# Retention's projections by seven half-block products in a stage of their own, and page keys gathered one unit ahead

## The chip, the cores and the metric

The kernel runs on one core of one Trainium2 chip. The core has five engines that work at the same time and wait for one another by semaphores: TensorE (PE in the profile, with its weight loads shown apart as PEld), VectorE (DVE), ScalarE (ACT), GpSimd (POOL) and SyncE (SP), which here only issues transfers. Each engine takes its own instructions strictly in their order. The metric is the time of one execution in microseconds on the device; smaller is better.

## What is computed

One step of a hybrid decoder layer on 1056 tokens: 1024 of a prompt and 32 of decoding (8 sequences of 4). All of it is float32. The part that matters here, cut from the reference:

```python
z = rmsnorm(x, ln_w) @ w_in                       # (1056, 1024) @ (1024, 9920)
rq, rk, rv, rg, cq, ckv, kr, mg, ga, gb = split(z)  # 1024, 1024, 2048, 2048, 384, 256, 64, 1024, 1024, 1024
rq = rope(rq by 4 heads of 256, pos)
rk = rope(rk by 4 heads of 256, pos) * 256 ** -0.5
rv = rv by 4 heads of 512
# retention, prompt: 8 chunks of 128 tokens per head, a state of 256 x 512 carried from chunk to chunk
scores = (q k^T) * decay_mask
o      = scores v + (q s_prev) * q_decay
s_new  = decay * s_prev + (k * k_decay)^T v
# latent attention of the decoding tokens: each sequence reads its 8192 past keys through a page table
c_past = cache_ckv[pt].reshape(-1, 256); r_past = cache_krope[pt].reshape(-1, 64)
p      = softmax([ql c_past^T + qr r_past^T, new tokens]);  o_lat = p [c_past, c_new]
```

Then come gates (`silu(rg)`, `silu(mg)`, `sigmoid(ga)`, `sigmoid(gb)`), three further projections, the prompt's latent attention and a last norm.

## The kernel before

**A product.** Float32 operands are split in two parts, high (`hi`) and low (`lo`), and `mac` (lines 262 to 268) multiplies them by three matmuls: high by high, high by low, low by high. `gemm` (line 270) makes one output tile of 128 columns of `w_in` by all 1056 tokens: three thirds of 352 tokens, each with 8 slices of the 1024 inputs, so 8 x 3 x 3 = 72 matmuls 352 wide, and it yields a cost of 0.441 after each `mac`. `load_w` fetches the tile's weights through two raw buffers (`wr`, 512 elements wide), casts them to `wh` on ScalarE or GpSimd and takes the low part `wl` on VectorE (`lo_of`, line 197); `wh` and `wl` have two buffers each. The normalised input `xn` stays in memory, 8 slices by high and low, until the projections are done.

**The stages.** In order: the input norm and the latents; the queries of the decoding tokens; the page attention (`page_attention`, line 672); retention (line 958 on); the prompt's latent attention; the last projections. The projections of the gates don't have a stage. They are a generator, `fill` (line 421), and `beside` (line 127) pours its matmuls between those of another stage in proportion to that stage's progress, counted in the costs that it yields; `woven` mixes two generators by their shares until both are used up. `fill` before: 8 tiles `ga`, 8 `gb`, 16 `rg`, 3 `mg` and the 4 `v` tiles of head 0, 39 in all.

**What sets the order.** The program is not run as it is written down. A planner takes all instructions with their dependences and buffers and sets each engine's order from its own estimate of times: the earlier one in the text has the higher priority, and a later one goes ahead where an engine would otherwise be free. On the chip that order is fixed, right or wrong. Buffers of one tag are handed on when their last reader is done.

**Page attention.** There are 16 units: two groups of four sequences, each by eight steps of 1024 keys (`past_keys`, line 612). A unit gathers its keys with 16 indirect transfers from GpSimd's queue (`gather`, line 579: two of the rotary keys into `rr` and two of the latent keys into `craw` for each sequence; each moves 128 rows). `craw` has buffers for two units under one tag, `rr` for one. Then 20 transposes on VectorE (`kt`, line 634, eight buffers, so two of five steps), 320 small score matmuls into one bank group `sc` (line 640), a maximum, an exponential on ScalarE, eight transposes, and the product with the keys (line 667). The unit yields 6.0 after its gathers, 12 in the scores, and 10.5 after.

**Retention.** q and k of head 0 are made first (`head_qk`), then for each head its v (`head_vg`), and then the head's recurrence (`prompt_chunks`, eight chunks with `front` and `back`) and its decoding state (`sample_state`) woven with q and k of the next head; beside the last head go five `mg` tiles. The rotation of q and k is done at the evacuation (lines 739 to 750). q, k and v of a head stay in memory, but for v of head 0, which goes through DRAM (`vD`).

Of the kernel before, what the change touches and what calls it, by code (L numbers as in the profile page):

```python
# [9 lines left out]
F32 = mybir.dt.float32  # L10
# [150 lines left out]
def decode_step(ctx: ExitStack, tc: tile.TileContext, A: dict, O: dict):  # L161
# [57 lines left out]
    vD = [dram.tile([P, NT], F32, tag=f"v{f}", name=f"v{f}") for f in range(4)]  # L219
# [197 lines left out]
    def chain(*gs):  # L417
        for g_ in gs:
            yield from g_

    fill = chain(gate_tiles(C_GA, gaD, range(8), AF.Copy), gate_tiles(C_GB, gbD, range(8), AF.Copy),
                 gate_tiles(C_RG, [t[:, f, :] for t in gtD for f in range(4)], range(16), AF.Silu), gate_tiles(C_MG, mgD, range(3), AF.Silu),
                 gate_tiles(C_RV, vD, range(4), AF.Copy))
# [53 lines left out]
    def big(name, shape, rows_=P):  # L477
        return p3.tile([rows_, *shape], F32, tag="craw", name=name, bufs=2 * NSEQ)
# [17 lines left out]
    def sample_queries():  # L496
# [11 lines left out]
        wk = big("wk", (2, HM, NOPE))  # L508
# [3 lines left out]
        qs = big("qq", (1536,))[:NR].rearrange("p (h d) -> p h d", h=HM)  # L512
        qq = big("qq", (768,))
# [19 lines left out]
        wkT = big("wkT", (HM, KL))  # L533
# [45 lines left out]
    def gather(b, jj, c, r):  # L579

        for i in range(NK):
            at_ = b * (NPG // 4) + NK * jj + i
            off = bass.IndirectOffsetOnAxis(ap=idx[:, at_:at_ + 1], axis=0)
            pool.indirect_dma_start(out=r[:, i], out_offset=None, in_=rows_r, in_offset=off)  # L584
            pool.indirect_dma_start(out=c[:, i], out_offset=None, in_=rows_c, in_offset=off)  # L585
# [26 lines left out]
    def past_keys(g, jj, st):  # L612
# [16 lines left out]
        for n, j in enumerate(steps):  # L629
            kt = []  # L630
            for s in range(NSEQ):
                t = ring("kt").rearrange("p (j k) -> p j k", j=2)
                src = keys[s][:, :, 32 * j:32 * j + 64] if j < 8 else rope[s]
                dve.transpose(t.rearrange("p j (n r) -> p n j r", r=32), src.rearrange("p n (j r) -> p n j r", r=32))  # L634
                kt.append(t)
            for i in range(2):
# [32 lines left out]
        dve.scalar_tensor_tensor(out=acc, in0=acc, scalar=corr, in1=pv[:, :KL], op0=ALU.mult, op1=ALU.add)  # L669
        yield 1.0  # L670

    def page_attention():
        state = [{}, {}]
        yield from new_tokens(0, state[0])
        for g in range(2):
# [5 lines left out]
            for jj in range(NPG // 4 // NK):  # L681
                yield from past_keys(g, jj, state[g])
# [36 lines left out]
    lph.close()  # L719

# [5 lines left out]
    tok = slots(p4, "tok", 8)  # L726
    cosR, sinR = (p4.tile([P, NT], F32, name=n) for n in ("cosR", "sinR"))
    sp.dma_start(cosR, A["ropeR"][:, 0, :])
    sp.dma_start(sinR, A["ropeR"][:, 1, :])
    lg = _log_g()  # L730

    def head_qk(h, X):
        for name, col in (("q", C_RQ), ("k", C_RK)):
            dst = X[name] = [(tok if h % 2 else qk4)(f"{name}{m}", dt=F32) for m in range(2)]

            def first(j, ps, sl, dst=dst):
                act.copy(dst[0][:, sl], ps)

            def second(j, ps, sl, dst=dst):
                x = wst.tile([P, TH], F32, tag="gev", name="rx", bufs=2)  # L740
                act.copy(x, ps)
                c, s = cosR[:, sl], sinR[:, sl]
                x0, x1 = dst[0][:, sl], dst[1][:, sl]
# [740 lines left out]
```

## Time and profile before

| | |
|---|---|
| median of 3 runs (lowest, highest) | 2253.39 us (2249.23, 2253.68) |
| the profiled execution: its time, its span | 2248.48 us, 2246.7 us |
| mean granted TensorE clock | 0.996 |
| TensorE busy in the span | 2192.1 us, 98% |
| VectorE, ScalarE, GpSimd busy | 1207.9, 709.8, 509.9 us |
| DMA traffic | 303.65 MB, mean 135 GB/s |

The profile's rows name a line, an engine, an operation, `out<-in` by the program's tile names with partitions x elements, and a count; then busy time, the mean of one in ns, and the engine's idle time before them with what ended it (`<-`). A timeline row is start, duration, engine, line. In rows of matmuls the duration is a model and neighbours overlap. A row by stretch gives the stretch, its length, the busy time of each engine with its count, the granted clock, the share of DMA time and GB/s. The page attention fills 204 to 806 us of the span, retention 806 to 1425.

### The profile page before, as it was taken

To read this page: it belongs to the slowest core of one execution; us is meant where nothing else is said; L and a number is where in the kernel's file an instruction comes from. 1 tells how busy PE (TensorE), PEld (TensorE's weight loads), DVE (VectorE), ACT (ScalarE), POOL (GpSimd) and SP (SyncE) were. 2 spreads that over 40 slices of the span, in tenths; PEclk is the share of its full clock that TensorE was granted. 3 is DMA by queue.
4 is the path that set the end of the run, shared out by engine and by line. 5 is a ranking of instruction groups with operands and counts; after the bars stand their busy time and mean duration, and the time that the engine had idled before them with its cause. 6 is when DMAs were issued, how large, how long until landed. Compare 5 with 4: busy or idle time off the path is not lost.

```text
span 2246.7 us, 45040 instructions
## 1 busy us (share of the span) xinstructions
PE 2192.1 (98%) x18482; PEld 1975.0 (88%) x18482; DVE 1207.9 (54%) x2624; ACT 709.8 (32%) x1532; POOL 509.9 (23%) x682
## 2 busy tenths in 40 slices
PE   8899999999999999999999999999999999999997
PEld 7898888888888899798798779888887999999997
DVE  5414454444544438728638447767767344454465
ACT  6312112222322123222222122355456332222243
POOL 2224434344444114203203102122222000000021
PEclk9999999999999999999999999999999999999999
DMA  8446565656565442532613753200110453333243
GB/s 234 131 148 247 184 223 174 227 183 222 182 232 178 153 135 59 165 99 66 212 49 95 237 162 87 81 23 24 37 46 27 149 192 106 96 94 107 87 141 114
DMA packets 293391, 303.65 MB, mean 135 GB/s; under 512 B 29760, under 2 KB 242048, under 8 KB 293184
## 3 DMA queue, kind: packets, MB, share of 16 engines
q1 hardware_dynamic: 268608, 216.86, 31.3%
q0 software_dynamic: 24576, 83.90, 10.8%
q8 instruction: 145, 2.38, 0.4%
q14 instruction: 62, 0.51, 0.1%
HBM read 234.76 MB, written 65.94 MB: 134 GB/s over the span
## 4 chain that ended last, share of the span: by engine, by line
PE 82%; DVE 7%; issue 6%; POOL 3%; ACT 2%; DMA 1%; SPq 0%; POOLq 0%; ACTq 0%; DVEq 0%
PE mm L266 19%; PE mm L268 18%; PE mm L267 18%; PE sc L640 5%; PE x L667 3%; PE mm L1199 2%; PE ac L267 2%; PE ac L268 2%; PE ac L266 2%; PE tr L1186 1%; PE ac L936 1%; PE ac L932 1%; DVE Stl L198 1%; PE ac L1139 1%; PE tr L791 1%
## 5 line engine op out<-in xcount | busy, mean ns | idle before, releaser
L266 PE MATMUL mm<-xh,wh 128*128 128x352 f32 x1728 | 577.4, 334 | 0.2 <-ACT qq L523 0.2
L268 PE MATMUL mm<-xh,wl 128*128 128x352 f32 x1728 | 562.4, 325 | 0.0
L267 PE MATMUL mm<-xl,wh 128*128 128x352 f32 x1728 | 560.5, 324 | 0.0
L266 PEld LDWEIGHTS mm<-xh,wh 128*128 128x128 f32 x1728 | 324.6, 188 | 38.4 <-issue 29.5
L268 PEld LDWEIGHTS mm<-xh,wl 128*128 128x128 f32 x1728 | 325.5, 188 | 18.6 <-issue 17.3
L267 PEld LDWEIGHTS mm<-xl,wh 128*128 128x128 f32 x1728 | 325.8, 189 | 14.5 <-issue 7.2
L198 DVE TENSOR_TENSOR wl<-wr,wh 128x512 fp32r<-128x512 f32 (+2 forms) x283 | 189.0, 679 | 202.4 <-ACT wh L247 175.7
L247 ACT CAST wh<-wr 128x512 fp32r<-128x512 f32 x248 | 149.8, 619 | 356.0 <-PE mm L267 319.2
L634 DVE STREAM_TRANSPOSE kt<-craw 128x512 f32<-128x512 f32 x256 | 159.3, 679 | 151.0 <-PE sc L640 150.4
L413 ACT ACTIVATE gev<-mm 128x352 f32<-128x352 f32 x132 | 61.1, 463 | 357.2 <-PE mm L268 256.7
L584 POOL DMA_INDIRECT rraw<-in_cache_krope_dram,idx x128 | 123.7, 966 | 215.4 <-DVE kt L634 166.2
L585 POOL DMA_INDIRECT craw<-in_cache_ckv_dram,idx x128 | 120.5, 941 | 142.6 <-PE x L667 102.2
L640 PE MATMUL sc<-kt,q 32*32 32x256 f32 x5120 | 125.5, 385 | 0.1
L266 PE MATMUL mm<-mh,wh 128*128 128x352 f32 x384 | 124.3, 324 | 0.8 <-DVE M L1309 0.8
L267 PE MATMUL mm<-ml,wh 128*128 128x352 f32 x384 | 124.5, 324 | 0.0
L268 PE MATMUL mm<-gh,wl 128*128 128x352 f32 x384 | 124.3, 324 | 0.0
L266 PE MATMUL mm<-gh,wh 128*128 128x352 f32 x384 | 124.3, 324 | 0.0
L268 PE MATMUL mm<-mh,wl 128*128 128x352 f32 x384 | 124.2, 324 | 0.0
L267 PE MATMUL mm<-gl,wh 128*128 128x352 f32 x384 | 124.1, 323 | 0.0
L1415 POOL TENSOR_TENSOR xr<-x1h,x1l 128x352 f32<-128x352 f32 x24 | 26.1, 1106 | 404.7 <-PE mm L268 367.0
L640 PEld LDWEIGHTS sc<-kt,q 32*32 32x32 f32 x5120 | 75.1, 103 | 34.0 <-issue 9.5
L1164 POOL TENSOR_SCALAR pr<-pr,rl 128x896 f32<-128x896 f32 (+3 forms) x64 | 49.7, 777 | 133.3 <-DVE rl L1163 91.0
(351 smaller groups left out, 4294.4 us busy)
## 6 DMA issues: line engine op xcount, KB each, us to landing
wr<-in_w_in_dram SPq DMA_DIRECT2D x144, 256.0 KB, 3.6
st<-in_state_ret_dram SPq DMA_DIRECT2D x32, 512.0 KB, 5.2
out_ret_sample_dram<-st SPq DMA_DIRECT2D x32, 512.0 KB, 3.3
wr<-in_w_ple_gate_dram SPq DMA_DIRECT2D x48, 256.0 KB, 3.0
gt<-gev SPq DMA_DIRECT2D x48, 176.0 KB, 3.3
gl<-go SPq DMA_DIRECT2D x16, 528.0 KB, 4.2
gate<-ga SPq DMA_DIRECT2D x16, 528.0 KB, 3.5
g<-gt SPq DMA_DIRECT2D x32, 256.0 KB, 3.2
```

The source lines that it names most:

```text
L198: dve.tensor_tensor(out=out, in0=src, in1=b32(hi), op=ALU.subtract)
L247: hi_by[0](hi, raw)
L266: pe.matmul(out, wh, xh, start=first, stop=False)
L267: pe.matmul(out, wh, xl, start=False, stop=False)
L268: pe.matmul(out, wl, xh, start=False, stop=last)
L413: act.activation(t, ps, func)
L584: pool.indirect_dma_start(out=r[:, i], out_offset=None, in_=rows_r, in_offset=off)
L585: pool.indirect_dma_start(out=c[:, i], out_offset=None, in_=rows_c, in_offset=off)
L634: dve.transpose(t.rearrange("p j (n r) -> p n j r", r=32), src.rearrange("p n (j r) -> p n j r", r=32))
L640: pe.matmul(sc[32 * s:32 * s + 32, q, :], Q["q4"][qs_, j + i, s, :], kt[s][qs_, i, :], start=n + i == 0, stop=n == NJ // 2 - 1 and i == 1, ...
L667: pe.matmul(pv[32 * s:32 * s + 32, :KL], pT[:, n, 32 * s:32 * s + 32], keys[s][:, n, :], start=n == 0, stop=n == 4 * NK - 1, tile_position ...
L1164: pool.tensor_scalar(p_[:, :W], p_[:, :W], rl, 1.0, op0=ALU.mult, op1=ALU.mult)
```

## The change

**Seven products for eight.** The projections of q, k and v leave retention for a stage of their own between page attention and retention. Each works on a pair of tiles (256 columns of `w_in`), and splits the 1024 inputs, the 256 columns and the 1056 tokens in halves. Four weight blocks and four token blocks would need eight products of blocks; Winograd's form of Strassen's method needs seven, with sums of blocks before and after. The sums of the tokens (`token_sums`, 32 GpSimd additions, 64 VectorE operations, 32 casts on ScalarE) are made once, the sums of the weights (`weights`) per pair. A block's product is 264 tokens wide (a quarter), with 4 slices of the inputs. Results leave PSUM through VectorE, ScalarE and GpSimd additions (`block`), q and k are rotated at that point with cosines fetched again for every quarter (`rotated`), and all of q, k and v goes to DRAM (`qkD`, `vD`). Retention loads them back chunk by chunk (`load_chunk`, `load_samples`).

**Fill.** It is now 8 `mg`, 16 `rg` and 4 `ga` tiles. The page stage's pacing goes from a budget of 455 to 198.4; what is left runs beside the token sums; the other 4 `ga` and 8 `gb` tiles go beside retention, whose heads are now one chain.

**Page keys.** A unit's gathers are issued while the unit before is scored: after the second and each later of its five steps those of one sequence, first both rotary, then both latent transfers. Their row indices are copied to a small tile on VectorE first. `craw` is split in two tags of four buffers, for even and odd units. The first yield of 6.0 falls away; the total that the pacing counts with, 16 x 36 + 10, stays.

```diff
-    fill = chain(gate_tiles(C_GA, gaD, range(8), AF.Copy), gate_tiles(C_GB, gbD, range(8), AF.Copy),
-                 gate_tiles(C_RG, ..., range(16), AF.Silu), gate_tiles(C_MG, mgD, range(3), AF.Silu),
-                 gate_tiles(C_RV, vD, range(4), AF.Copy))
+    fill = chain(gate_tiles(C_MG, mgD, range(8), AF.Silu),
+                 gate_tiles(C_RG, ..., range(16), AF.Silu),
+                 gate_tiles(C_GA, gaD, range(4), AF.Copy))
...
-    def past_keys(g, jj, st):
-        seqs = [4 * g + s for s in range(NSEQ)]
-        rr = [p3.tile([P, 2, NK, 4 * ROPE], F32, tag="rr", name="rraw", bufs=2) for _ in range(2)]
-        cr = [big("craw", (NK, 4 * KL)) for _ in seqs]
-        for s, b in enumerate(seqs):
-            gather(b, jj, cr[s], rr[s // 2][:, s % 2])
-        yield 6.0
+    def past_keys(now, nxt, st):
+        _, _, cr, rr = now
+        coming = None
         for n, j in enumerate(steps):
             (four transposes)
+            if n and nxt:
+                if coming is None:
+                    coming = keys_of(*nxt)
+                gather(coming, n - 1)
             (64 score matmuls)
...
-    beside(page_attention(), 16 * 36 + 10, fill, 455)
+    beside(page_attention(), 16 * 36 + 10, fill, 16 * 12.4)
     gph.close()
     open_banks()
-    run(fill)
     ph.close()
+    def weights(raws, out):
+        a11, a12, a21, a22 = raws
+        wh, wl = wtiles()
+        for n, raw in enumerate((a11, a12)):
+            out.append(split(raw, wh[:, n * HK:(n + 1) * HK], wl[:, n * HK:(n + 1) * HK]))
+            yield
+        dve.tensor_tensor(out=a11, in0=a21, in1=a11, op=ALU.subtract)
+        dve.tensor_tensor(out=s2, in0=a22, in1=a11, op=ALU.add)
+        operand(s2)
+        dve.tensor_tensor(out=a12, in0=a12, in1=s2, op=ALU.subtract)
+        yield
+        dve.tensor_tensor(out=a21, in0=a21, in1=a22, op=ALU.add)
+        for raw in (a21, a11, a22, a12):
+            operand(raw)
+            yield
+    def block(evac, parts, W, s_, done):
+        bank, x = ((mm, X11), (tr, X21), (mm, T[1]), (ac, T[0]), (mm, T[2]), (tr, T[3]), (ac, X22))[n]
+        o = bank()[:, :QT]
+        for k in range(HK):
+            mac(o, (W[n][0][:, k, :], W[n][1][:, k, :]), x(k), k == 0, k == HK - 1)
+        (block 0: kept; 1, 2, 4, 5, 6: added to earlier ones on VectorE; 3: kept, and one sum on GpSimd)
+    run(woven((first_operands(), 15.0), (fill, 36.0)))
+    raws = quadrants(pairs[1][0])
+    for n, (_, evac) in enumerate(pairs):
+        coming = []
+        more = weights(raws, coming) if n + 1 < len(pairs) else iter(())
+        for s_ in range(2):
+            parts, done = {}, []
+            for i in range(7):
+                block(evac, parts, W, s_, done)
+                if (i in (1, 2, 4, 5)) if s_ == 0 else (i in (3, 4, 5)):
+                    next(more, None)
+        if n + 2 < len(pairs):
+            raws = quadrants(pairs[n + 2][0])
+        run(more)
+        W = coming
...
-    run(head_qk(0, X))
-    for h in range(HR):
-        run(head_vg(h, X))
-        ...
+    heads = chain(prompt_chunks and sample_state of each head; the last head's in reverse)
+    run(woven((heads, 4 * 43.5), (chain(fill, 4 ga tiles, 8 gb tiles), 12 * 10.6)))
```

More of the change, by code (lines that the diff above doesn't have):

```diff
@@ L673, in page_attention @@
         state = [{}, {}]
+        units = [(g, jj) for g in range(2) for jj in range(NPG // 4 // NK)]
+        keys = keys_of(*units[0])
+        for s in range(NSEQ):
+            gather(keys, s)
         yield from new_tokens(0, state[0])
@@ L722, in decode_step @@
+    ph.close()
     qph = ctx.enter_context(ExitStack())
```

254 lines of the change are left out of this document (173 added, 81 removed).

## The prediction

> **What bounds the kernel now.** I read the head of the page first, then the busy time by stage, then the spacing of matmuls.
>
> ```profile
> span 2246.7 us, 45040 instructions
> PE 2192.1 (98%) x18482; PEld 1975.0 (88%) x18482; DVE 1207.9 (54%) x2624; ACT 709.8 (32%) x1532; POOL 509.9 (23%) x682
> PE 82%; DVE 7%; issue 6%; POOL 3%; ACT 2%; DMA 1%; SPq 0%; POOLq 0%; ACTq 0%; DVEq 0%
> ```
>
> The span is TensorE work: 98% busy, and 82% of the chain that ended last. Only 54.6 us of the span are without a matmul. So work taken from TensorE shortens the run, unless a new stage leaves it waiting.
>
> ```profile
> 204.00:806.00 602.00, 601.95 (x8716) 510.70 (x8715) 278.25 (x471) 139.75 (x254) 219.23 (x231) 1.00 0.58 189
> 806.00:1425.00 619.00, 603.06 (x3519) 533.50 (x3518) 379.93 (x901) 164.03 (x334) 138.80 (x204) 1.00 0.41 127
> ```
>
> The first stretch is the page attention, the second retention (columns: stretch, its length, busy time of PE, PEld, DVE, ACT, POOL, then clock, DMA share, GB/s). The first has no idle TensorE at all, the second 16 us (2.6%) with its other engines at their tightest. That 2.6% is my yardstick for a stage that is packed closely.
>
> **The price of a matmul.** The modelled duration of one (324 ns) is no price, as matmuls overlap; the distance of starts is.
>
> ```profile
> 1759.73 0.33 PE L267 MATMUL mm<-ml,wh 128*128 128x352 f32 x1
> ...
> 1761.98 0.32 PE L266 MATMUL mm<-mh,wh 128*128 128x352 f32 x1
> ```
> ```profile
> 1496.11 0.64 PE L1199 MATMUL mm<-pth,v 128*128 128x256 f32 x4
> 1496.58 0.39 PE L1199 MATMUL mm<-ptl,v 128*128 128x256 f32 x2
> 1496.81 0.63 PE L1199 MATMUL mm<-pth,v 128*128 128x256 f32 x4
> 1497.28 0.40 PE L1199 MATMUL mm<-ptl,v 128*128 128x256 f32 x2
> 1497.52 0.31 PE L1139 MATMUL ac<-k,q 128*128 128x320 f32 x1
> ```
>
> At 352 columns 14 starts take 2.25 us: 0.1608 us each. At 256 columns 12 take 1.41 us: 0.1175. The line through both (0.45 ns a column) gives 0.121 us at 264.
>
> **Part 1, seven products for eight.** Before, 32 output tiles of q, k and v take 8 x 3 x 3 = 72 matmuls of 352: 2304 x 0.1608 = 370.5 us. After, 16 column pairs take 2 halves x 7 blocks x 4 x 3 = 168 matmuls of 264: 2688 x 0.121 = 325.3 us. Gain 45.2 us, all on the bounding engine. That is one eighth, 46 us, less the fixed part of more, shorter matmuls.
>
> What must hide beside a pair (168 x 0.121 = 20.3 us):
>
> ```profile
> L198 DVE TENSOR_TENSOR wl<-wr,wh 128x512 fp32r<-128x512 f32 x256 | 176.0, 700 | 194.7 <-ACT wh L247 175.7 <-POOL wh L195 18.6
> L746 DVE TENSOR_TENSOR k<-rx,cosR 128x352 f32<-128x352 f32 x12 | 6.2, 516 | 2.6 <-ACT rx L741 2.6
> L247 ACT CAST wh<-wr 128x512 fp32r<-128x512 f32 x248 | 149.8, 619 | 356.0 <-PE mm L267 319.2 <-issue 15.2 <-DMA wr<-in_w_ple_gate_dram 12.4
> L750 POOL TENSOR_TENSOR q<-q,rt x12: 928/943/1398, 819.9 to 1203.0; 128x352 f32<-128x352 f32 x12
> L745 DVE TENSOR_TENSOR rt<-k,sinR x12: 508/526/1277, 829.2 to 1250.3; 128x352 f32<-128x352 f32 x12
> wr<-in_w_in_dram SPq DMA_DIRECT2D x144, 256.0 KB, 3.6
> ```
> ```profile
> 904.57 0.57 SPq L246 DMA_DIRECT2D wr<-in_w_in_dram  x1
> ```
>
> By the line through the first two rows an add of 264 elements on DVE costs 0.42 us; POOL's 0.943 us scales to 0.71 (estimates). Weights need 4 combinations and 7 low parts of 512: 11 x 0.70 = 7.7 us of DVE. Evacuation is 6 adds a half, the rotation 8 more: a q or k pair costs DVE 7.7 + 28 x 0.42 = 19.5 us and POOL 10 x 0.71 = 7.1, a v pair 7.7 + 12 x 0.42 = 12.7 and 1.4. DVE's mean is 16.1 us in 20.3, under 80%, and the pairs alternate. Eight PSUM banks let TensorE run some six blocks (9 us) ahead of a late evacuation. The casts go to ACT (7 x 0.62 us a pair), which is idle for two thirds of the span. Each pair's four loads are issued behind the stores of the pair before on SP; at 3.6 us to landing they come within the first third of the 20.3. An add that waits for a load holds DVE's queue, evacuations included; the banks cover that. Bounds: 0, to 50 us (rival C). I take the yardstick, 2.6% of 325: 8.5 us.
>
> **Part 2, the first operands.** They come after the page stage, because their pool takes its memory. 32 POOL sums x 0.71 = 23 us, 64 DVE operations x 0.42 = 27 us and the first weights' 7.7: up to 58 us if nothing overlaps. The cover is fill: 28 tiles x 24 x 0.441 = 296 cost units, less 36 and 24 in the stages before, less what the page stage pours. Without its first yield a unit yields 22.5, so the stage reaches 370 of the 586 that the pacing expects: 125 are poured and not 198. That leaves 111 units, 10.5 tiles, 122 us of matmuls for 58 us of operands. The first operand holds one of two weight buffers, though, so some nine tiles load into a single one: a cast and a low part, 0.62 + 0.70 us, between tiles: 12 us if nothing else runs there. Bounds 0 to 58; I take 8 us, nearest to those two rows, as the new stage's own blocks can fill some of the gaps.
>
> **Part 3, the page stage.** Its fill shrinks, so its own rhythm shows.
>
> ```profile
> 204.00:806.00 602.00, 258.69 (x800) 150.66 (x799) 1.00 0.58 189
> ```
> ```profile
> 657.70 0.94 POOL L585 DMA_INDIRECT craw<-in_cache_ckv_dram,idx  x1 [7.33 <-PE x L667]
> ...
> 666.41 0.94 POOL L585 DMA_INDIRECT craw<-in_cache_ckv_dram,idx  x1 [0.30 <-issue]
> ```
> ```profile
> DMA to landing us min/median/max: 4.3/7.8/9.0
> ```
> ```profile
> 608.22 0.71 DVE L634 STREAM_TRANSPOSE kt<-craw 128x512 f32<-128x512 f32 x1 [3.04 <-PE sc L640]
> 608.85 1.19 DVE L645 TENSOR_REDUCE nb<-sc 128x1 f32<-128x1024 f32 x1
> 609.96 0.69 DVE L634 STREAM_TRANSPOSE kt<-craw 128x512 f32<-128x512 f32 x1
> 610.58 0.14 DVE L648 TENSOR_TENSOR nm<-nm,nb 128x1 f32<-128x1 f32 x1
> 610.64 1.29 DVE L634 STREAM_TRANSPOSE kt<-craw 128x512 f32<-128x512 f32 x2
> ...
> 615.75 0.69 DVE L662 COPY pT<-x 128x512 f32<-128x512 f32 x1
> ```
>
> One of the three fill lines has 800 matmuls here, so the fill is 2400 x 0.1608 = 386 us and the stage's own work 602 - 386 = 216, or 13.5 us in each of 16 units of 37.6. After, a unit gets 198.4 x 22.5/586 = 7.6 cost units, 17.3 products of three matmuls, 8.3 us: TensorE needs 21.8 us a unit. POOL issues 16 gathers a unit, 7 starts in 8.71 us, 1.244 each: 19.9 us. Before, that stood in 37.6 us and hardly mattered; now POOL has 1.9 us to spare, and the last gather of a sequence lands at least 4.3 us after issue. The one-ahead order and the sequence per step keep POOL from standing behind one late buffer. The 64 index copies are new: at the 0.14 us of the nm row above 9 us of DVE, which is busy for 278 of 602 us; I cost them at nothing. But they add a wait: four gathers stand on POOL behind a copy that stands on DVE behind a step's transposes.
>
> ```profile
> L652 ACT ACT_TABLE_LOAD x10 | 12.8, 1283 | 17.1 <-DVE nm L648 17.0
> 617.36 3.66 PE L667 MATMUL x<-craw,pT 128*32 128x256 f32 x64
> ```
> ```profile
> 806.52 0.45 ACT L737 COPY q<-mm 128x352 f32<-128x352 f32 x1
> ```
>
> Silu fill now meets the softmax's Exp in every unit: 16 table loads there for 10, 6 x 1.28 us of later softmax, inside the bounds below. (The second row, the unit's last products, serves rival B.) And fill is not bound to its place: the third row evacuates the first query tile, emitted behind the page stage, so its matmuls ran before the stage's end. The order planner takes later fill where it sees TensorE free, up to the 122 us left. So TensorE loses only where the planner misjudges a gather. Bounds 0 to 16 x 5 us (rival B); by the same yardstick 2.6% of 16 x 21.8 = 349: 9 us.
>
> **Part 4, retention.** It loses its projections and reads q, k and v back.
>
> ```profile
> 860.00:912.00 52.00, 50.31 (x298) 46.12 (x297) 44.85 (x113) 14.87 (x32) 20.32 (x31) 1.00 0.26 72
> g<-gt SPq DMA_DIRECT2D x32, 256.0 KB, 3.2
> ```
>
> In a chunk phase DVE is 86% busy. The rotation leaves it and some fill leaves TensorE; both shrink, and I keep the 16 us of idle: 0, between -10 and +15. A chunk's two loads have the shape of the gate's, 3.2 us to landing, and are asked one chunk (over 8 us) ahead; uncovered they would cost 32 x 3.2 us. SP gets 64 of them, and in the new stage up to 16 transfers a pair, 9 us of issue in 20.3; DMA was at 0.41 and 0.58 of its time. What is new (17 MB written, 17 MB read back, rotation tables again and again, less the v tiles of head 0) makes some 38 MB; at the second stretch's rate (127 GB/s at 0.41, so 310) that is 122 us over stages of 700: it fits.
>
> **Sum**, against the profiled execution's 2248.5 us: -45.2 + 8.5 + 8 + 9 = -19.7, so 2229. The median of the runs shown, 2253.4, lies 0.2% above that execution; splitting the offset I say 2231.
>
> **Rivals.**
> B, slower: the page stage runs on the gathers. The row order above shows DVE turning the next unit's keys ahead of this unit's pT copy. If that order stays, the copy waits for the last gather: from one unit's end 14 gathers (17.4 us; two can go before), landing 4.3, then turn 0.7, copy 0.7 and products 3.7, 26.8 us a unit for 21.8. That is 16 x 5 = 80, less the 9 counted: 2300; at half of it 2260. For it: the 1.9 us of slack. Against: the changed gather order, and fill that can move in. It decides from 1.8 us of idle a unit: 45.2 - 8.5 - 8 = 28.7 over 16.
> C: the new stage runs on DVE and POOL. The row of L745 shows it: 526 ns in the median and 1277 at most, beside POOL's adds. If all their work excludes each other, a q or k pair takes 19.5 + 7.1 = 26.6 us for 20.3, so 8 x 6.3 = 50 more, less 8.5: 2272. It decides from 3.5 us a q or k pair. Against: most pairs of operations don't meet, and v pairs are light. The Trainium skill ("SBUF — State Buffer", section "Who interferes with whom") says that a DVE instruction with two SBUF inputs and a GpSimd instruction that reads SBUF exclude each other for a whole instruction. By that rule rival C's sum is the one to use for two-input work; the row's maximum, more than twice its median, agrees, but its median shows that they meet rarely.
> D: the fill is used up in the page stage, and the operands stand bare: 58 - 8 more, 2279.
> E: shorter matmuls don't come cheaper at 264, some other floor holds at 0.1608: 2688 x 0.1608 = 432, 107 us more, 2336. Break-even is 370.5/2688 = 0.138 us. The 256-column rows speak against it.
>
> **How the numbers follow.** The forecast has 0.47 (own range 2207 to 2246), B 0.27, C 0.12, D 0.08, E 0.06. A run tells 0.2% (4.5 us) from no change. Faster: nearly all of the forecast's share and the mild ends of B, C and D, 0.52; within 0.2%: 0.06; slower: 0.42. The low end is the bare gain, 2253 - 45; the high end takes in the full B and leaves out E and what mishaps add up: 2305.
>
> **What would show it.** Right: starts 0.121 us apart in the new stage, pairs of 20 to 21 us; page units of 22 us with TensorE busy; no hole longer than a few us between the last page product and the first block. Wrong: sc matmuls waiting for DVE kt, and kt for the gathers, in every unit (B); blocks waiting for DVE or POOL adds in q and k pairs (C); a hole with POOL sums in it (D); a spacing above 0.138 us (E). Retention with more than 30 us of idle would refute part 4.

## The result, and the profile after

The changed kernel takes 2397.6 us (median of 4 runs, 2392.9 to 2406.5) beside 2253.1 us for the kernel before (2249.2 to 2253.7): a ratio of 1.065, with a 95% interval of 1.061 to 1.069. The forecast was 2231 us and faster, with 2305 as its high end; the run is 144 us slower than the kernel before.

The head of the page and its clock row, for the profiled execution of 2392.9 us:

```profile
span 2390.9 us, 47239 instructions
PE 2244.4 (94%) x18866; PEld 1966.0 (82%) x18866; DVE 1392.3 (58%) x3060; ACT 753.7 (32%) x1594; POOL 565.7 (24%) x734
PEclk9999888888999999999999999999999999999999
```

TensorE was to have 45 us less to do. Instead it is busy for 52 us more, is idle for 146.5 us where it was idle for 54.6, and its clock falls below full speed in slices 5 to 10, which lie in the page attention. The busy time by stage, with the same columns as before (stretch, length, PE, PEld, DVE, ACT, POOL, clock, DMA share, GB/s), for page attention, first operands, first operands with the new stage, and retention:

```profile
204.00:674.00 470.00, 414.17 (x7121) 283.99 (x7116) 258.54 (x485) 105.49 (x163) 216.99 (x229) 0.87 0.57 190
674.00:725.00 51.00, 38.11 (x208) 36.44 (x208) 44.93 (x75) 19.52 (x49) 28.09 (x32) 0.86 0.18 55
725.00:1167.00 442.00, 429.95 (x3258) 424.96 (x3258) 255.94 (x508) 106.12 (x214) 93.13 (x96) 0.99 0.40 117
1167.00:1570.00 403.00, 373.18 (x2025) 289.73 (x2024) 283.16 (x732) 116.60 (x229) 75.50 (x127) 1.00 0.71 211
```

From 1570 us on the two kernels are alike (821 us to the end in both). So the miss of 164 us in the span lies in these four rows. The forecast made 358 us of the first (16 x 21.8, plus 9): 112 more were measured. It made 464 of the second and third (325.3 for the blocks, 122 for the fill that is left, 8.5 and 8 of idle time): 493 were measured, 29 more. Its sum leaves 380 for the last, which is 403, 23 more.

The page stage is where to look first. The chain of the last products (L677) runs from 228.7 to 670.3 us, 15 intervals of 29.4 us where 21.8 were forecast. Its waits (engine and line, what it waited for, total, times, longest):

```profile
POOL rraw L594 <- DVE kt L640: 120.6, 16, 11.2
DVE rows L590 <- DMA craw<-in_cache_ckv_dram,rows: 86.3, 35, 4.3
PEld sc L650 <- DVE kt L640: 79.0, 66, 4.7
PE sc L650 <- DVE kt L640: 53.3, 28, 4.3
DVE kt L640 <- PE sc L650: 26.8, 28, 2.1
DVE kt L640 <- DMA craw<-in_cache_ckv_dram,rows: 1.6, 1, 1.6
```

The scores wait for the transposes, and the transposes hardly ever wait for their keys (1.6 us, once; another 27 us is for the scores of an earlier step). What waits for the landing of gathers, 86 us in all, is the small index copy. The timeline of VectorE, and of TensorE in the same microseconds, shows how they hang together:

```profile
397.25 0.17 DVE L590 COPY rows<-idx 128x2 int32<-128x2 int32 x1 [1.41 <-DMA craw<-in_cache_ckv_dram,rows]
401.25 0.17 DVE L590 COPY rows<-idx 128x2 int32<-128x2 int32 x1 [3.83 <-DMA craw<-in_cache_ckv_dram,rows]
401.36 2.49 DVE L640 STREAM_TRANSPOSE kt<-craw 128x512 f32<-128x512 f32 x4
```
```profile
394.12 2.83 PE L650 MATMUL sc<-kt,q 32*32 32x256 f32 x64 [2.81 <-DVE kt L640]
...
402.13 2.33 PE L650 MATMUL sc<-kt,q 32*32 32x256 f32 x58 [4.29 <-DVE kt L640]
404.38 0.66 PE L267 MATMUL mm<-xl,wh 128*128 128x352 f32 x1
404.85 0.49 PE L268 MATMUL mm<-xh,wl 128*128 128x352 f32 x1
405.14 0.49 PE L266 MATMUL mm<-xh,wh 128*128 128x352 f32 x1
...
406.82 0.33 PE L266 MATMUL mm<-xh,wh 128*128 128x352 f32 x1
406.98 0.32 PE L267 MATMUL mm<-xl,wh 128*128 128x352 f32 x1
```

A copy of 0.17 us stands for 3.83 us at the head of VectorE's queue until a gather for the next unit has landed, because the four buffers of the index tile are all taken by gathers under way. The four transposes behind it belong to the unit at hand and their keys are there; they go as soon as the copy is through. TensorE has stood still for 4.29 us by then, and comes back at half its rate: the fill's matmuls start 0.29 us apart (404.85, 405.14) where at 406.82 they are 0.16 apart again. The clock had fallen one wait earlier: the granted clock is 1.00 up to 392.8 us, goes to 0.50 at about 393, within the wait of 2.81 us that ends at 394.12, and is back at 1.00 by 406.8.

The Trainium skill ("TensorE: Matmul & The Clock Gate", section "HAM oscillation — how this bites in real kernels") says that waits of more than about 3.4 us drop TensorE's clock and that a loop with such a wait in each round pays the drop each time. The trace agrees that the drop is paid again and again, with a granted clock of 0.87 over the stage; it differs in the length, as the drop above came within a wait of 2.81 us. The same 5120 score matmuls are busy for 177.4 us (first row) where the kernel before has 125.5 (second row):

```profile
L650 PE MATMUL sc<-kt,q 32*32 32x256 f32 x5120 | 177.4, 445 | 53.4 <-DVE kt L640 53.3
L640 PE MATMUL sc<-kt,q 32*32 32x256 f32 x5120 | 125.5, 385 | 0.1
```

### The profile page after: what moved, and what is told of

Same layout as the page of the kernel before. It is cut to its first block, busy times and chain, and to the rows that moved or that the text cites. A ratio compares the mean times of both kernels' runs of the same rounds, so it can differ in the third digit from the quotient of the medians.

```text
span 2390.9 us, 47239 instructions
## 1 busy us (share of the span) xinstructions
PE 2244.4 (94%) x18866; PEld 1966.0 (82%) x18866; DVE 1392.3 (58%) x3060; ACT 753.7 (32%) x1594; POOL 565.7 (24%) x734
## 5 line engine op out<-in xcount | busy, mean ns | idle before, releaser
L266 PE MATMUL mm<-xh,wh 128*128 128x352 f32 (+1 forms) x1088 | 368.9, 339 | 10.8 <-ACT gev L413 5.8
L267 PE MATMUL mm<-xl,wh 128*128 128x352 f32 (+1 forms) x1088 | 358.3, 329 | 0.0
L268 PE MATMUL mm<-xh,wl 128*128 128x352 f32 (+1 forms) x1088 | 356.9, 329 | 0.0
L266 PEld LDWEIGHTS mm<-xh,wh 128*128 128x128 f32 x1088 | 212.2, 195 | 47.8 <-issue 28.3
L650 PE MATMUL sc<-kt,q 32*32 32x256 f32 x5120 | 177.4, 445 | 53.4 <-DVE kt L640 53.3
L267 PEld LDWEIGHTS mm<-xl,wh 128*128 128x128 f32 x1088 | 212.6, 195 | 14.7 <-issue 11.0
L268 PEld LDWEIGHTS mm<-xh,wl 128*128 128x128 f32 x1088 | 211.8, 195 | 14.3 <-issue 13.0
L247 ACT CAST wh<-wr 128x512 fp32r<-128x512 f32 x184 | 110.0, 618 | 321.9 <-PE mm L267 269.2
L594 POOL DMA_INDIRECT rraw<-in_cache_krope_dram,rows x128 | 123.0, 961 | 179.8 <-DVE kt L640 128.0
L594 POOL DMA_INDIRECT craw<-in_cache_ckv_dram,rows x128 | 120.2, 939 | 74.9 <-issue 35.7
L266 PE MATMUL mm<-mh,wh 128*128 128x352 f32 x384 | 124.2, 323 | 1.0 <-DVE M L1462 1.0
L266 PE MATMUL mm<-gh,wh 128*128 128x352 f32 x384 | 124.3, 324 | 0.0
L819 POOL TENSOR_TENSOR b<-b,b 128x264 f32<-128x264 f32 x32 | 32.8, 1024 | 216.3 <-DVE b L819 155.4
```

The lines of the kernel that those rows point to most:

```text
L247: hi_by[0](hi, raw)
L266: pe.matmul(out, wh, xh, start=first, stop=False)
L267: pe.matmul(out, wh, xl, start=False, stop=False)
L268: pe.matmul(out, wl, xh, start=False, stop=last)
L594: pool.indirect_dma_start(out=out[:, i], out_offset=None, in_=src, in_offset=off)
L650: pe.matmul(sc[32 * s:32 * s + 32, q, :], Q["q4"][qs_, j + i, s, :], kt[s][qs_, i, :], start=n + i == 0, stop=n == NJ // 2 - 1 and i == 1, ...
```

## Experiments: the page stage

Each is set beside runs of the kernel before on the same chip, 2251.8 to 2253.1 us in all but the last two experiments. Theory 1 is that the copies' wait at the head of VectorE's queue does the harm. Theory 2 is that the loop of gathers, landing and key buffers does it (rival B). Theory 3 is that some wait is always there, and only the missing fill lays it bare.

**More buffers for the index tile.**

```diff
-        rows_ = p3.tile([P, NK], I32, tag="rows", name="rows", bufs=4)
+        rows_ = p3.tile([P, NK], I32, tag="rows", name="rows", bufs=16)
```

> One size is changed: the small index tile has 16 buffers instead of 4, so that a copy of indices on VectorE never has to wait for the landing of the gathers of one unit before. Theory 1 (this wait, at the head of VectorE's queue, holds the transposes of the keys and through them the scores and the next gathers): page units of 22 to 25 us instead of 29.4, the run at 2285 to 2335 us instead of 2397.6. Theory 2 (the loop of gather issue on GpSimd, landing, transposes and the products that free the key buffers sets the rhythm, whatever the copies do): units of 26.8 us, 16 x 2.6 = 42 us less, 2355. Theory 3 (the stage lacks fill, and some wait or other always stays bare): no change within 10 us.

Measured: 2377.8 us, 1.056 (1.053 to 1.058) of the kernel before; units of 28.4 us ((655.6 - 230.0)/15). None of the three had this. The copies still wait, as the row of the first shows, and the second shows why (first and last start of all 64 copies; the gathers go on to 621 us):

```profile
397.03 0.35 DVE L590 COPY rows<-idx 128x2 int32<-128x2 int32 x1 [2.99 <-DMA craw<-in_cache_ckv_dram,rows]
...
L590 DVE COPY rows<-idx x64: 124/169/372, 156.1 to 531.1; 128x2 int32<-128x2 int32 x64
```

The last copy is now made 90 us, some three units, ahead of the last gathers; with 4 buffers it came at 613.9. The planner makes each copy as early as it takes a buffer to be free, so 16 buffers move the copies three units ahead, and many of them (36 of 64 wait) again ask for a buffer whose gather is just under way. The edit didn't take the wait away, and so doesn't speak against theory 1. A buffer for each of the 64 copies was not tried.

**No copies.**

```diff
-        rows_ = p3.tile([P, NK], I32, tag="rows", name="rows", bufs=4)
-        dve.tensor_copy(rows_, idx[:, at_:at_ + NK])
...
-                off = bass.IndirectOffsetOnAxis(ap=rows_[:, i:i + 1], axis=0)
+                off = bass.IndirectOffsetOnAxis(ap=idx[:, at_ + i:at_ + i + 1], axis=0)
```

> The changed kernel without its 64 index copies: the gathers read their row numbers from the index table itself, still one unit ahead and one sequence per step. With 16 buffers the copies still waited, since they were put four units ahead; here there is nothing left that could wait. Theory 1 (the copies' wait at the head of VectorE's queue is the fault): units of 22 to 25 us instead of 29.4, the run at 2270 to 2320 us, level with the 2279.6 of the old gathers. Theory 2 (the gather loop, with the key buffers split by even and odd units, is the fault): units of 26.8 us or more, the run at 2345 to 2390.

Measured: 2293.4 us, 1.018 (1.015 to 1.020): 104 of the 144 us come back by taking out 64 copies that are busy for 11 us. Units take 23.3 us ((572.9 - 224.0)/15). The page stage of this kernel:

```profile
204.00:578.00 374.00, 370.13 (x7119) 261.93 (x7117) 250.37 (x428) 105.54 (x163) 215.97 (x228) 1.00 0.71 240
```

The gathers are the same 16 a unit on the same queue, one unit ahead; TensorE has 4 us of idle time in 374, at full clock. Theory 1 stands, theory 2 falls.

**The copies on GpSimd.**

```diff
-        dve.tensor_copy(rows_, idx[:, at_:at_ + NK])
+        pool.tensor_copy(rows_, idx[:, at_:at_ + NK])
```

> The same copies with the same four buffers and so the same waits, but issued by GpSimd instead of VectorE. Theory 1 (what costs is the place of the wait, ahead of transposes on VectorE): nearly all comes back, 2275 to 2325 us, with GpSimd's copies waiting for the landings in VectorE's stead. If it is the wait itself, wherever it stands (the gathers of the next unit cannot be issued before those of this unit have landed), little comes back: 2360 to 2400.

Measured: 2355.5 us, 1.046 (1.044 to 1.047), units of 27.1 us. It falls between the two, nearer to the second. The waits of this kernel's page stage:

```profile
POOL rows L590 <- DMA craw<-in_cache_ckv_dram,rows: 81.2, 36, 4.0
...
DVE kt L640 <- DMA craw<-in_cache_ckv_dram,rows: 68.4, 33, 3.5
```

The wait of 81 us is now on GpSimd, where the gathers stand behind it, and the transposes wait for late keys. So of 104 us that the copies cost, 42 come from the place on VectorE and 62 from a wait in either queue. A wait for a landing ahead of the transposes or ahead of the gathers is in the loop both times.

**The gathers alone, with all the fill.** The kernel before with the new gathers and copies, and a pacing that still pours all of its fill beside the page stage:

```diff
-    beside(page_attention(), 16 * 36 + 10, fill, 455)
+    beside(page_attention(), 16 * 36 + 10, fill, 570)
```

> The other half alone: the kernel before with the new gathers; the pacing is set to 570 so that all of its fill is still poured beside the page stage (37.6 us of matmuls a unit). Theory 3 (the wait exists but only a lack of fill lays it bare): the page stage stays at 602 to 615 us and the run at 2250 to 2270. Theory 1 in its strict form (a wait of this kind cannot be filled, as scores and fill stand in one fixed order): 16 x 3 to 16 x 7.6 us more, 2300 to 2375. A gain from the earlier gathers would show as less than 2245.

Measured: 2312.1 us, 1.026 (1.024 to 1.029). The stage:

```profile
204.00:866.00 662.00, 630.74 (x8691) 522.64 (x8690) 289.97 (x530) 141.58 (x258) 220.03 (x230) 0.96 0.52 171
```

With 37.6 us of matmuls for each unit TensorE still has 31 us of holes and 662 us for 602. So fill doesn't cover this wait: TensorE's order is fixed, scores stand in it ahead of fill, and the fill behind them can't pass. Theory 3 falls in its plain form.

**More fill beside the changed page stage.**

```diff
-    beside(page_attention(), 16 * 36 + 10, fill, 16 * 12.4)
+    beside(page_attention(), 16 * 36 + 10, fill, 16 * 19.6)
```

> The waits stay and the fill changes: the pacing of the page stage is given 16 x 19.6 cost units instead of 16 x 12.4, so that about 198 are poured beside it and not 125; 73 of them, about 80 us of matmuls, leave the stretch of the first operands. Theory 3 (the waits cost because nothing covers them): the page stage grows from 470 us by no more than 25, the stretch behind it shrinks from 156 by 60 or more, the granted clock of the page stage rises from 0.87 to 0.95 or more, and the run is at 2320 to 2350 us. Rival D of the prediction (the 38 cost units that are left, 42 us of matmuls, no longer hide up to 58 us of operands): a hole appears behind the page stage and the run stays at 2370 to 2400. Theory 1 in its strict form (a unit takes 29.4 us because of the copies and has about 3.5 us of idle TensorE): 16 x 3.5 = 56 us of the 80 are taken in, 2340.

Measured: 2373.2 us, 1.054 (1.051 to 1.056). The 161 more products of three matmuls (443 for 282), 78 us, lengthen the stage by 60, so it takes in 18 of them. The scores' waits for the transposes are still 46.8 us, for 53.3. This is in the band of rival D, but not by its mechanism alone: most of the gain is missing in the page stage already.

## Experiments: the seven products and the stage of their own

**The change without its new gathers.** The page attention of the kernel before, everything else as changed. Its unit yields 28.5, so it pours 355 products for 282.

```diff
-    def past_keys(now, nxt, st):
+    def past_keys(g, jj, st):
...
+        for s, b in enumerate(seqs):
+            gather(b, jj, cr[s], rr[s // 2][:, s % 2])
+        yield 6.0
```

> The change without its second half: the projections by seven products in their own stage, but the page attention gathers as before, straight from the index table, all 16 transfers at the head of a unit, one tag of eight key buffers. A unit again yields 28.5, so about 154 cost units of fill are poured beside the page stage: TensorE's need is 216 + 154 x 1.09 = 384 us. Theory 1 (the new gathers with their copies are at fault): a page stage of 390 to 420 us, and the run at 2270 to 2320. Theories 2 and 3 (the page stage with less fill runs on gather, landing and transposes in either scheme): units of 26.8 us or more, a stage of 430 to 470 us, and the run at 2340 to 2390.

Measured: 2279.6 us, 1.012 (1.009 to 1.014). Its page stage takes 400 us for a need of 387. That is what theory 1 said. It is also the finding that matters for the forecast's sign: without the copies the change is still slower than before.

**Eight products in a stage of their own.** The same kernel, with q, k and v by whole output tiles as before (72 matmuls of 352 each), written out and read back, without token sums and first operands:

```diff
-    run(woven((first_operands(), 15.0), (fill, 36.0)))
-    (the 16 pairs by seven products)
+    run(fill)
+    for h in range(HR):
+        run(head_qk(h))
+        run(gate_tiles(C_RV + h * DV, [vD[h][:, f, :] for f in range(4)], range(4), AF.Copy))
```

> On the version with the old gathers (2279.6 us): q, k and v are computed in their own stage as there and written out, but by the eight products of the kernel before (output tiles of three times 352 columns) and without token sums and first operands. It tells what the stage of its own costs from what seven products bring. TensorE's need is 45 us more. If the stage of its own is what costs (page stage 13 us and retention 38 us over TensorE's need, as in the version with the old gathers) and the seven products give back in their operands and stage 40 of their 45 us, the run is at 2275 to 2290 us. If seven products bring their 45 us less some 10, it is at 2305 to 2320. If the losses of retention come from the seven products' operands and traffic, and the stage of its own is free, it is at 2250 to 2260.

Measured: 2290.9 us, 1.017 (1.015 to 1.019), just above the first of the three. So moving the projections out of retention, with the fill dealt out anew and q, k and v read back, costs 39 us by itself (2251.8 before), and seven products for eight bring back 11 and not 45. Some 13 of the 39 lie in the page stage, which takes 400 us for a need of 387 here too; most of the rest is retention's. Loads of q, k and v that come late aren't seen there: this row is all that TensorE itself waits for transfers in the retention of this kernel, and it is for the state.

```profile
PEld ac L961 <- DMA st<-in_state_ret_dram: 1.9, 4, 1.0
```

The stretch from the page stage's end to the last projection, with seven products first (of the kernel with the old gathers) and then with eight:

```profile
604.00:1056.00 452.00, 427.13 (x3224) 421.61 (x3224) 296.70 (x576) 118.38 (x247) 121.34 (x128) 0.97 0.38 114
```
```profile
604.00:1064.00 460.00, 460.00 (x2838) 460.00 (x2838) 120.14 (x179) 96.32 (x201) 53.04 (x49) 1.00 0.35 106
```

With eight products TensorE is full: 942 products of three at 0.1608 us, 454 us in 460. With seven it should need 413 (175 products of fill, 84 us, and 2688 block matmuls at 0.1224, 329) and takes 452. The 39 us of loss are 25 us of idle time and 14 of slowed matmuls. Of them 21 lie in the first 56 us, beside the token sums, and 18 in the 16 pairs.

**The token sums on VectorE.** In the operand stretch of the changed kernel the low parts of the token sums are slow (the first row), beside GpSimd's additions:

```profile
L198 DVE TENSOR_TENSOR Tl<-c,Th 128x264 fp32r<-128x264 f32 x32 | 23.3, 786 | 0.0
```

```diff
-                    pool.tensor_tensor(out=b[name], in0=b32(xn[kk][0][:, sl]), in1=b32(xn[kk][1][:, sl]), op=ALU.add)
+                    dve.tensor_tensor(out=b[name], in0=b32(xn[kk][0][:, sl]), in1=b32(xn[kk][1][:, sl]), op=ALU.add)
```

> On the version with the old gathers: the 32 sums of the high and low parts of the tokens go from GpSimd to VectorE. In the operand stretch VectorE's two-input work beside GpSimd takes 788 to 914 ns where alone it takes 420. If that exclusion sets the stretch, 32 x 0.42 = 13 us more on VectorE are paid by 16 us less of slowed rows and by the hops that fall away: the stretch of 56 us shrinks by 5 to 12 and the run is at 2268 to 2275. If something else sets it (fill tiles that wait for their weight buffer, evacuations behind the operands on ScalarE), no change: 2275 to 2285.

Measured: 2280.3 us against 2279.6, no change. The rows of this kernel:

```profile
L198 DVE TENSOR_TENSOR Tl<-c,Th 128x264 fp32r<-128x264 f32 x32 | 11.8, 430 | 1.1 <-ACT Th L729 1.1
L743 DVE TENSOR_TENSOR b<-xh,xl 128x264 f32<-128x264 f32 x32 | 11.7, 429 | 4.1 <-PE x L701 4.1
```

The exclusion of rival C is real in this stretch: 786 ns beside GpSimd, 430 without, as the Trainium skill has it ("SBUF — State Buffer", section "Who interferes with whom"). But the sums cost VectorE 11.7 us and the freed rows give 11.5 back, so nothing moves.

**Four gate tiles moved into retention** (on the kernel with the old gathers):

```diff
-                 gate_tiles(C_RG, ..., range(16), AF.Silu),
-                 gate_tiles(C_GA, gaD, range(4), AF.Copy))
+                 gate_tiles(C_RG, ..., range(16), AF.Silu))
...
-    run(woven((heads, 4 * 43.5), (chain(fill, 4 ga tiles, 8 gb tiles), 12 * 10.6)))
+    run(woven((heads, 4 * 43.5), (chain(fill, 8 ga tiles, 8 gb tiles), 16 * 10.6)))
```

> On the version with the old gathers (2279.6 us): four gate tiles, 42 cost units or 46 us of matmuls, are moved from the fill of the page stage and of the first operands into retention, which had lost most of its cover (its stretch is about 398 us there, some 38 of them more than TensorE needs). If lack of cover is what retention pays for, it grows by 46 us less 10 to 20, and the operand stretch, with 37 cost units left, loses 0 to 20: 2260 to 2280. If retention's waits stand in a fixed order that fill doesn't enter, retention grows by the full 46 us and the run is at 2280 to 2300.

Measured: 2266.4 us, 1.006 (1.005 to 1.008), the best version found, still behind the kernel before. The stretch from the last block to the first `mh` product (first start, last start of two groups of L266), with old gathers alone and then with the four tiles moved:

```profile
L266 PE MATMUL ac<-xh,Wh x128: 278/284/289, 657.0 to 1054.6; 128*128 128x264 f32 x128
L266 PE MATMUL mm<-mh,wh x384: 318/323/430, 1768.2 to 2142.1; 128*128 128x352 f32 x192
```
```profile
L266 PE MATMUL ac<-xh,Wh x128: 278/284/405, 654.7 to 1001.5; 128*128 128x264 f32 x128
L266 PE MATMUL mm<-mh,wh x384: 318/323/427, 1751.9 to 2126.1; 128*128 128x352 f32 x192
```

It is 713.6 us (1768.2 - 1054.6) and 750.4: 37 more for 46 us of fill, so retention lost 9 us less, just under what the first sentence asked for. Another 7 of the 16 us between these two executions were won ahead of it.

**Three further edits of that version.** The first pair's operands out of the fill's weight buffers; the gathers ahead without copies, at the same fill of 155 cost units; both together:

```diff
-        wh, wl = wtiles()
+        wh, wl = wtiles() if out is not W else (None, None)
...
+            if out is W:
+                operand(raw)
```

> On the version with old gathers and four gate tiles moved (2266.4 us): the first pair's first two weight operands go to the ring of seven instead of one of the two weight buffers that the fill tiles use, so that fill in the operand stretch has both. If the fill there waits for its one weight buffer, the stretch from the page stage's end to the last block loses 10 to 15 us less: 2250 to 2257. If its holes come from blocks placed ahead of their operands in TensorE's fixed order, no change: 2262 to 2270.

> The gathers one unit ahead without copies, with the four gate tiles moved into retention and the pacing set so that about 155 cost units are poured beside the page stage, as with the old gathers. If the earlier gathers are worth something once nothing waits in VectorE's queue, units take 24.0 to 24.4 us instead of 24.8 and the run is at 2253 to 2262; if the early and the late gathers are alike, 2263 to 2270.

> The last two together. If both theories of the weight buffer and of the earlier gathers hold, 2238 to 2252 us, ahead of the kernel before (2253); if neither does, 2262 to 2270.

Measured: 2268.5, 2269.3 and 2268.1 us, no change in any. So the holes beside the first operands don't come from the one weight buffer. And gathers one unit ahead are worth nothing at equal fill: the 14 us between the kernel without copies (2293.4) and the one with the old gathers (2279.6) came with the smaller fill, 125 cost units for 157.

**Retention's share in the mix.** The mixing of retention and fill calls retention 4 x 43.5 cost units, while its yields add up to 4 x 47.6, and the fill ends 31 us before retention does. On the version with four tiles moved, 4 x 52 and 4 x 47.7; then 4 x 52 with eight products, and with all edits:

```diff
-    run(woven((heads, 4 * 43.5), ...
+    run(woven((heads, 4 * 52), ...
```

> On the version with old gathers and four gate tiles moved (2266.4 us), one number is changed: the share of retention in the mix with the fill is 4 x 52 instead of 4 x 43.5. If the fill is poured too fast and retention's end stands without cover, the last gate products move from 31 us before retention's end to within 10 us of it, and the run is at 2246 to 2256 us. If the cover is too thin everywhere, what the end wins the earlier chunks lose: 2262 to 2270.

> The same with 4 x 47.7, what retention's yields add up to. If the end without cover is the cause, about half to all of the gain of the share 52: 2248 to 2260 us, with the last gate products 10 to 20 us before the end. If not, 2262 to 2270.

> The share 4 x 52 on the version with eight products in their own stage (2290.9 us). If the early end of the fill is the cause of retention's part of the 39 us, 10 to 25 us come back: 2265 to 2280. If the cover is too thin, no change: 2286 to 2295.

> All parts together: gathers one unit ahead without copies, 155 cost units beside the page stage, four tiles moved, the first pair's operands in the ring, and the share 4 x 52. If the early end of the fill is the cause, 2246 to 2258 us, level with the kernel before or ahead of it; if not, 2262 to 2270.

Measured: 2272.6, 2268.3, 2284.6 and 2268.8 us. The last gate products moved to the end as meant (1443.7 us with 4 x 52, for 1412.0), and the time didn't: what the end won, the chunks ahead lost. Only with eight products 6 us came back, fewer than the 10 that the first of its sentences asked for.

**The chain of the group norm.** Retention's largest named wait on TensorE, in the version with four tiles moved, was that of the normed chunk's transposes for ScalarE:

```profile
PE tr L931 <- ACT on L920: 11.4, 23, 2.4
```

Once they were written one step later, and once the norm's scale and shift were left out:

```diff
-            yield from due
             for cost in u:
                 if cost is None:
                     break
                 yield cost
+            yield from due
             due = u
```
```diff
-        act.activation(on[:n], po, AF.Identity, bias=nb[:n], scale=s[:n])
+        act.copy(on[:n], po)
```

> On the version with old gathers and four gate tiles moved (2266.4 us): in retention the transposes of a chunk's normed output are written behind the products of the next chunk and not ahead of them, so that the normalisation has one step more to finish. If this wait is retention's loss, 5 to 12 us come back: 2254 to 2261. If it is only where thin cover shows, the wait moves elsewhere and the run stays at 2262 to 2270.

> On the same version, the normed output is a plain copy of the chunk's output instead of the scaled and shifted one: the group norm's scale and shift of the retention output are left out (its statistics are still taken), so the transposes wait for ScalarE's copy alone and not for the chain through VectorE and GpSimd. If the chain is retention's loss, the wait of 11 us goes and the run is at 2250 to 2258 us; if not, 2262 to 2270.

Measured: 2531.5 and 2528.8 us, beside 2447.1 us for the kernel before on that chip; the totals say nothing, as the kernel before took some 190 us more there than in every other comparison. The traces of these two place it in the page stage: units of 41 us, with transposes waiting for something outside the core's engines (204 us put down to "remote" in each of them); what that is, the traces don't tell. Behind the page stage they can be read: from the last block's matmul to the first `mh` product it took 750.4 us in the version with four tiles moved; it takes 750.1 with the later transposes and 742.8 without scale and shift:

```profile
L266 PE MATMUL ac<-xh,Wh x128: 278/284/323, 921.0 to 1268.6; 128*128 128x264 f32 x128
L266 PE MATMUL mm<-mh,wh x384: 318/323/433, 2018.7 to 2392.6; 128*128 128x352 f32 x192
```
```profile
L266 PE MATMUL ac<-xh,Wh x128: 278/284/289, 924.2 to 1275.6; 128*128 128x264 f32 x128
L266 PE MATMUL mm<-mh,wh x384: 318/323/429, 2018.4 to 2392.4; 128*128 128x352 f32 x192
```

Asking later changes nothing, and without the chain 7.6 us come back of some 30 that retention takes there beyond TensorE's need. The chain is a part of retention's loss and not the whole of it. The rest stays open: no single wait of the trace holds it, and no edit here brought it back.

No version beats the kernel before.

## Why the prediction was wrong

The step that failed is in part 3: "The 64 index copies ... I cost them at nothing. But they add a wait: four gathers stand on POOL behind a copy that stands on DVE behind a step's transposes." The wait was looked for in one direction only, the gathers behind the copy. The copy itself waits, for a buffer that is free only when a gather has landed, and the transposes stand behind it. Priced from the rows, it was there to be seen: four buffers are one unit's copies, a landing takes 4.3 to 9 us, and VectorE's queue is in order. It costs 104 us.

Point by point:

- **Part 1, the price of a block's matmul: right.** 0.121 us forecast, 0.122 measured (53 starts from 999.80 to 1006.27 us). Rival E is out.

```profile
999.80 0.28 PE L267 MATMUL mm<-Tl,Wh 128*128 128x264 f32 x1
...
1006.27 0.28 PE L266 MATMUL mm<-xh,wh 128*128 128x264 f32 x1
```

- **Parts 1 and 2, what stands idle there: mis-sized.** 8.5 and 8 us forecast, 39 measured with the old gathers. The 8 for the operands were some 21: "nearest to those two rows" took single cast and low-part rows for a stretch in which VectorE is busy for 45 of 51 us and sums, casts and fill follow one another in fixed orders (51 us in the changed kernel, 56 with the old gathers). The 8.5 for the pairs were about 18; some 10 of them are waits of TensorE for PSUM banks, which take its results, until ScalarE (5.6 us) or VectorE (4.1) has emptied them. The share of idle time in the stages of before was no measure for this one.
- **Part 3, the fill: right in amount, wrong in its freedom.** 125 cost units were poured, as worked out (282 products). "The order planner takes later fill where it sees TensorE free" didn't happen: the count is the same with the copies' waits and without them, which fits a planner that foresaw no idle time there; its estimates aren't on record.
- **Part 3, the gathers: right.** GpSimd's 16 gathers and their landing are nearly hidden once the copies are gone: 23.3 us a unit, 21.8 forecast, with TensorE busy for 370 of 374 us. Rival B gave the sign and the row (scores waiting for `kt` in every unit), with another cause and 71 of the 112 us.
- **Part 4, retention: wrong.** "I keep the 16 us of idle". The text named both that fill leaves TensorE and that VectorE is at 86% there, and took them to cancel. Retention takes 403 us in the changed kernel for some 362 of need: before, both stages needed 602 + 619 - 16 = 1205; seven products need 41 less (370.5 - 329), and 352 (page stage) and 450 (fill and blocks) are spent ahead. Of the 41 us, 30 are idle time (29.8, just at the edge of what the text gave as its sign of being wrong); the others are matmuls that are slowed or packed loosely. The run with eight products shows that this comes with moving the projections out and not with the seven products.
- **Rivals C and D.** Blocks of pairs wait little (430 of 442 us busy behind the first operands), so C's 50 us are out there; D is there in part, with 13 of 51 us idle and the rest at 0.86 of the clock.
- **The sum's sign: wrong even without the copies.** Measured on the path from before: the stage of its own +39, seven products -11, the smaller fill with the early gathers +14, the copies +104: 146, where the difference is 144 (the kernel before varies by 1 us from chip to chip). The forecast had the first at 0, the second at about -29 and the rest at 9.

The same account in words: before, the projections were matmuls that could lie between anything, and they filled the holes of retention. In a stage of their own they meet no holes at all (460 of 460 us busy with eight products), and what they used to cover stands open. That reading is argued and not shown: four gate tiles put back into retention as cover brought 9 us there, of some 40, and what holds the rest is open.

## What to carry to other kernels

Ask of every small instruction that a change adds what it waits for, and who stands behind it in its queue; a copy of 0.17 us into a ring of buffers that DMAs read is a wait for their landing, and more buffers help little where a planner hands them out early (16 for 4 gave 20 us of the 104). Matmuls that can go anywhere may be worth more as cover than their own time: before taking them out of a stage, count what they hide there. A saving on the bounding engine is to be set against the idle time of the stage that brings it, measured from a stage with the same work and not from another's share.

## What was not expected of the hardware

TensorE can come back from a wait as short as 2.7 us at a lower rate. In the kernel with 16 index buffers the granted clock is 1.00 before such a wait, falls to 0.50 within it, and stays there until about 410 us; 64 score matmuls take 2.83 us behind it, and 1.67 some 12 us later:

```profile
397.90 2.83 PE L650 MATMUL sc<-kt,q 32*32 32x256 f32 x64 [2.67 <-DVE kt L640]
...
410.10 1.67 PE L650 MATMUL sc<-kt,q 32*32 32x256 f32 x64
```

In the changed kernel's page stage this and the waits cost about alike: 56 us of idle time and some 60 of slowed matmuls, in 470 us for 352 of need. And in one session the kernel that took 2249 to 2260 us in every other comparison took 2441 to 2452. The two traces taken in that session, of versions of the changed kernel, have their loss in the page attention, where keys are gathered by index; of the kernel before there is no trace from it, and what made it slow isn't known.
